# Handing the selection and the gates to the scheduler at 2.4 instead of 0.8 per attention step

## The chip, the cores and the metric

The kernel runs on one core of a Trainium2 chip. The metric is the device time of one execution in microseconds (us). The core's engines each work through an instruction queue of their own: TensorE (PE, with its weight loads as PEld), VectorE (DVE), ScalarE (ACT), GpSimd (POOL), and SyncE (SP), which here only issues transfers.

## What is computed

One encoder layer on 512 tokens of width 1024, in float32 throughout. Only the parts that stand near the change are told in detail.

```python
hn = rms_norm(h, g_mix)
c_q, c_kv, k_r, q_d, k_d, v_d = jnp.split(hn @ w_in, offs, axis=-1)
o_mla = mla_attention(...)          # 8 heads, full softmax over 512 keys
o_dil = dilated_attention(...)      # 8 heads, three dilated windows joined by their log sums
h = h + concat(rms_norm(o_mla), rms_norm(o_dil)) @ w_out
xn = rms_norm(h, g_ffn)
# PEER: per token and head two products with 128 keys each, top 16 of each,
# top 16 of the 256 sums, softmax: 8 x 16 experts out of 16384, with gates g
a = gelu(einsum('td,thkd->thk', xn, u_tab[eidx]))
h = h + einsum('thk,thkd->td', g * a, v_tab[eidx])
h = h + sigmoid(rms_norm(h, g_ple) @ w_gate) * (p @ w_proj)
out = rms_norm(h, g_final)
```

## The kernel before

The 512 tokens are four token tiles of 128. Tiles 1, 2 and 3 are "dense": for them all 16384 experts are computed, in 128 steps of 128 experts, and each hidden value is multiplied by a gate that is zero for experts that were not chosen. Tile 0 is the "gather" tile: its 128 chosen rows per token are fetched with indirect transfers and worked on by VectorE beside the dense steps.

The program has four stages in time:

1. The projections (to about 150 us in the trace).
2. The attention. A group is two heads of one token tile; there are 8 groups for a tile, 32 in all, in the tile order 1, 2, 3, 0. The generator `attention()` issues for each group the scores (L422 or L425), then the product with the values for the group three before (L466), the transposes for the group two before (L451) and the scaling of the weights, and yields after each of these four steps. After every yield the loop at L786 takes one step of `after(t)`, the work that follows a tile's attention, and then calls `fill(us)`.
3. `after(t)`: the output projection (L523, `mm<-wq,mT`), two adds per half into `ht` (L528), the norm (`ss`, a power on GpSimd at L141, then `hn`, L538 or L536), the transposes of `hn` (L545) with their copies `xTt`, the query projection (L562, `mm<-xTt,wq`), and the key products (L574), whose result `sc` goes to the selection. When it is through, it puts the tile's selection and, for a dense tile, four chunks of gates on the list `bg`.
4. The dense steps: hidden (L870, `h`), gelu and gates, values (L896, `y`). Steps 0 to 11 do tiles 1 and 2 only, while the gates of tile 3 are still being built; from step 12 on each step does three tiles, written out in a fixed order by hand.

The list `bg` is first in, first out. Its entries are generators: `topk(t)`, the selection (almost all on VectorE: maxima L589 and L598, their places L592 and L601, removal L595, the candidates L622, then the decoding and the one-hot products from L632 to L641; at its end three transposes on TensorE, L669 and L670), and `gates(t, c)`, which builds for 32 tokens the 128 by 128 table of gates: `hot` (L709) and `B` (L713) on VectorE for 8 tokens, 16 products on TensorE (L724), two copies into `stage` on ScalarE (L727), and at the end of a chunk one transfer of 2 MB to memory (`gD`, L729). `hot`, `B` and `stage` have two buffers each, and the products go to two PSUM buffers.

`fill(us)` takes steps from the head of `bg` until the costs that they name use up `us`. Those costs (1.6 for eight tokens of gates, for example) are numbers in the code, not measured times. A scheduler then orders the instructions of each engine, by the order in which the program issued them and by what is ready in its own model; on the chip every engine keeps that order. Two rules pull work forward whatever the rate is: three buffers `sc` exist, so `after` calls `fill` until enough halves of a selection are picked (L568), and before the dense steps everything on `bg` up to the gates of tile 3 is issued (L841). The gates of tile 3 are held back until then (`PRE`, `barred`).

Of the kernel before, what the change touches and what calls it, by code (L numbers as in the profile page):

```python
# [56 lines left out]
KE = 12  # L57
END = 10
NE, NX = 2, 4
FILL_A, FILL_B, FILL_D = 0.8, 3, 2  # L60
FILL_E = 2.2
PRE = ("gates", ORDER[2], 0)
ED = 2, 1, 0, 0
# [1146 lines left out]
```

## Time and profile before

| what | value |
|---|---|
| median of 3 runs | 1672.45 us (1669.31 to 1672.63) |
| the profiled execution's own time | 1674.36 us |
| span of that execution in the trace | 1672.3 us |
| TensorE busy | 1604.1 us (96% of the span) |
| VectorE busy | 1223.8 us (73%) |
| ScalarE busy | 737.5 us (44%) |
| GpSimd busy | 372.6 us (22%) |

The span is what the trace covers; the execution's own time is 2.06 us longer. Times in the trace count from the span's start. An engine's idle time is put down to the instruction that it waited for; matmuls are pipelined, so the start of one to the start of the next is its price, and the printed duration is longer. The granted clock of TensorE has two levels in this trace, 1.2 and 2.4 GHz, shown as 0.50 and 1.00.

### The profile page before, as it was taken

How to read it: one execution, taken by the hardware profiler on the slowest of the kernel's cores; microseconds unless marked ns; L12 is line 12 of the kernel's file. 1: busy time of each engine (PE TensorE's matmuls, PEld its weight loads, DVE VectorE, ACT ScalarE, POOL GpSimd, SP SyncE). 2: the span in 40 equal slices, each digit the busy share in tenths (PEclk: the TensorE clock that was granted, in tenths of full speed). 3: DMA queues.
4: the chain of work that ended last, by engine and by line, in shares of the span. 5: the costliest groups of instructions: out<-in, count | busy, mean ns of one | idle time of the engine just before them, and what ended most of it. 6: DMA issues, size and time to landing. Idle time of an engine off the chain costs nothing.

```text
span 1672.3 us, 24854 instructions
## 1 busy us (share of the span) xinstructions
PE 1604.1 (96%) x9369; PEld 1405.3 (84%) x9369; DVE 1223.8 (73%) x2495; ACT 737.5 (44%) x1220; POOL 372.6 (22%) x302
## 2 busy tenths in 40 slices
PE   7999999999679989999999999999999999999998
PEld 6776777778669889999999999999999999999877
DVE  5235468796999867787887887788888888864566
ACT  5435655645446544433333333333333333333455
POOL 1000000000000001044444444444444444300000
PEclk9999999999889999999999999999999999999999
DMA  7212254375867667599999999999999999975511
GB/s 240 62 52 95 82 172 133 114 239 206 298 248 243 233 216 265 185 309 327 324 321 323 309 334 321 324 316 339 320 312 313 334 322 323 319 269 200 182 58 51
DMA packets 154088, 402.73 MB, mean 241 GB/s; under 512 B 13168, under 2 KB 64496, under 8 KB 152432
## 3 DMA queue, kind: packets, MB, share of 16 engines
q1 hardware_dynamic: 115232, 241.48, 43.4%
q0 software_dynamic: 36864, 134.23, 23.3%
q10 hardware_dynamic: 1872, 25.43, 3.9%
q8 instruction: 73, 1.20, 0.3%
q14 instruction: 47, 0.39, 0.1%
HBM read 369.64 MB, written 31.46 MB: 240 GB/s over the span
## 4 chain that ended last, share of the span: by engine, by line
PE 82%; DVE 11%; ACT 2%; DMA 2%; issue 1%; POOL 1%; SPq 0%; POOLq 0%; DVEq 0%; ACTq 0%
PE y L896 31%; PE h L870 31%; PE mm L194 4%; PE mm L523 2%; PE mm L562 2%; PE pg L965 2%; PE po L466 2%; PE gq L724 2%; DVE B L713 1%; PE tp L451 1%; PE mm L425 1%; PE mm L422 1%; PE tp L250 1%; DVE rep L595 1%; DVE hot L709 1%
## 5 line engine op out<-in xcount | busy, mean ns | idle before, releaser
L870 PE MATMUL h<-xTh,lo 128*128 128x384 f32 (+1 forms) x1024 | 340.3, 332 | 0.8 <-ACT gt L673 0.8
L870 PE MATMUL h<-xTh,hi 128*128 128x384 f32 (+1 forms) x1024 | 340.1, 332 | 0.0
L870 PE MATMUL h<-xTl,hi 128*128 128x384 f32 (+1 forms) x1024 | 339.0, 331 | 0.0
L774 POOL DMA_INDIRECT row<-in_u_dram,ei x128 | 165.9, 1296 | 449.2 <-DVE row L762 241.4
L896 PE MATMUL y<-hi,wl 128*128 128x512 f32 x768 | 241.4, 395 | 8.5 <-DVE wl L885 8.5
L896 PE MATMUL y<-lo,wh 128*128 128x512 f32 x768 | 238.9, 392 | 0.0
L896 PE MATMUL y<-hi,wh 128*128 128x512 f32 x768 | 238.4, 392 | 0.0
L774 POOL DMA_INDIRECT row<-in_v_dram,ei x128 | 182.5, 1426 | 208.5 <-DVE h L768 170.1
L819 DVE TENSOR_TENSOR lo<-v,hi 128x1024 fp32r<-128x1024 f32 x140 | 171.5, 1225 | 73.4 <-ACT hi L817 72.8
L879 ACT ACTIVATE w<-h 128x384 f32<-128x384 f32 (+2 forms) x140 | 65.0, 464 | 361.6 <-PE h L870 346.6
L870 PEld LDWEIGHTS h<-xTh,lo 128*128 128x128 f32 x1024 | 193.8, 189 | 5.8 <-ACT gt L673 1.1
L870 PEld LDWEIGHTS h<-xTl,hi 128*128 128x128 f32 x1024 | 193.8, 189 | 4.7
L870 PEld LDWEIGHTS h<-xTh,hi 128*128 128x128 f32 x1024 | 193.5, 189 | 0.0
L819 DVE TENSOR_TENSOR lo<-u,hi 128x1024 fp32r<-128x1024 f32 x128 | 156.8, 1225 | 46.0 <-ACT hi L817 44.5
L817 ACT ACTIVATE hi<-v 128x1024 fp32r<-128x1024 f32 x140 | 148.2, 1058 | 94.2 <-PE y L896 94.0
L896 PEld LDWEIGHTS y<-lo,wh 128*128 128x128 f32 x768 | 144.7, 188 | 32.3
L896 PEld LDWEIGHTS y<-hi,wh 128*128 128x128 f32 x768 | 144.6, 188 | 31.7
L896 PEld LDWEIGHTS y<-hi,wl 128*128 128x128 f32 x768 | 141.3, 189 | 30.4 <-DVE wl L885 9.8
L768 DVE SCALAR_TENSOR_TENSOR h<-row,hh,h 128x1024 f32<-128x1024 f32 x128 | 164.2, 1283 | 2.9
L762 DVE SCALAR_TENSOR_TENSOR row<-row,xg 128x1024 f32<-128x1024 f32 x128 | 150.2, 1221 | 0.0
L883 ACT ACTIVATE wh<-w 128x384 fp32r<-128x384 f32 (+2 forms) x140 | 69.6, 497 | 180.4 <-DVE w L881 179.0
L817 ACT ACTIVATE hi<-u 128x1024 fp32r<-128x1024 f32 x128 | 133.9, 1046 | 1.6 <-PE h L870 1.6
(255 smaller groups left out, 2249.5 us busy)
## 6 DMA issues: line engine op xcount, KB each, us to landing
u<-in_uT_dram SPq DMA_DIRECT2D x140, 512.0 KB
v<-in_vB_dram SPq DMA_DIRECT2D x140, 512.0 KB
gD<-stage ACTq DMA_DIRECT2D x12, 2048.0 KB
g<-gD SPq DMA_DIRECT2D x29, 768.0 KB
wq<-in_w_out_dram SPq DMA_DIRECT2D x32, 512.0 KB
wq<-in_w_pq_dram SPq DMA_DIRECT2D x32, 512.0 KB
w<-in_w_in_dram SPq DMA_DIRECT2D x24, 256.0 KB
wg<-in_w_gate_dram SPq DMA_DIRECT2D x8, 512.0 KB
```

What stands on the lines that cost most here:

```text
L194: nc.tensor.matmul(acc[t], l[:, c, tok[t]], r, start=(c == 0 and k == 0), stop=(c == NC - 1 and k == 2))
L466: nc.tensor.matmul(cx[t]["po"][a * HD:(a + 1) * HD, hp, :], vv[:, grp, c, h * HD:(h + 1) * HD], st[g][a][:, c, :], start=(c == 0), stop=(c ...
L523: nc.tensor.matmul(pss[grp][:, q * P:(q + 1) * P], mT[grp][:, c, :], w[:, grp * 4 + c, :], start=(c == 0), stop=(c == 3))
L762: nc.vector.scalar_tensor_tensor(row, row, 1.0, xg, op0=OP.mult, op1=OP.mult, accum_out=hh[:, k:k + 1])
L768: nc.vector.scalar_tensor_tensor(h0, row, hh[:, k:k + 1], h0, op0=OP.mult, op1=OP.add)
L774: nc.gpsimd.indirect_dma_start(out=row, out_offset=None, in_=v if w else u, in_offset=bass.IndirectOffsetOnAxis(ap=eis[s][:, kk:kk + 1], a ...
L817: nc.scalar.activation(hi, w, AF.Copy)
L819: nc.vector.tensor_sub(lo, w, hi.bitcast(F32))
L870: nc.tensor.matmul(ps, l[:, cs], r[:, c, ts], start=(c == 0 and k == 0), stop=(c == NC - 1 and k == 2))
L879: nc.scalar.activation(w, ps, AF.Gelu)
L883: nc.scalar.activation(wh, w, AF.Copy)
L896: nc.tensor.matmul(y[n][s], l[:, ts], r[:, s * 512:(s + 1) * 512], start=(first and k == 0), stop=(last and k == 2))
```

## The change

One number: the budget with which `fill` is called after every step of the attention goes from 0.8 to 2.4.

```diff
 KE = 12
 END = 10
 NE, NX = 2, 4
-FILL_A, FILL_B, FILL_D = 0.8, 3, 2
+FILL_A, FILL_B, FILL_D = 2.4, 3, 2
 FILL_E = 2.2
 PRE = ("gates", ORDER[2], 0)
```

No instruction is added or removed; 140 weight tables, 768 gate products and all selections are the same. What changes is where they stand in each engine's queue. From tile 1's selection to the first dense steps the queues differ; before that, and from dense step 12 on, they read alike.

TensorE, where the normalised rows of token tile 2 are transposed (`hn`). `po` is the value product of the attention, `tp` the transposes of its weights, `mm<-xTt,wq` the query projection. Before:

```order
L466 MATMUL po<-prT,vv 64x128 x8
L545 MATMUL tp<-ident,hn 128x128 x8
L451 MATMUL tp<-ident,pr 128x128 x4
L562 MATMUL mm<-xTt,wq 128x128
```

And now (`gq<-ident,i1t` and `gq<-ident,gd` are the transposes that end the selection of tile 1, `gq<-hot,B` its gate products):

```order
L669 MATMUL gq<-ident,i1t 128x128 x2
L670 MATMUL gq<-ident,gd 128x128
L425 MATMUL mm<-kd,qd 128x512
L466 MATMUL po<-prT,vv 64x128 x8
L545 MATMUL tp<-ident,hn 128x128 x8
L724 LDWEIGHTS B
L724 MATMUL gq<-hot,B 128x128
```

Of the last two rows there are 80 pairs before the next transposes of the attention; then the attention, the query projection and the rest of the 256 gate products alternate. Before, the gate products of tile 1 began only a tile later, behind the attention of tile 0. The same pattern now comes a second time, for tile 2, after the transposes of tile 3.

VectorE at the same place, around `hn` of tile 2. `ss` leads to the norm, `xTt` are the two copies of its transposes, `e`, `ga`, `hot` and `B` belong to the gates. Before:

```order
L140 TENSOR_SCALAR ss<-ss 128x1
L538 TENSOR_SCALAR hn<-ht,ss 128x1024
L158 TENSOR_TENSOR xTt<-tp,gc 128x512 x2
L442 RECIPROCAL sm<-sm 128x2
L434 ISA pr,sm<-mm,bias_t 128x512
```

And now:

```order
L709 TENSOR_TENSOR hot<-ioh,ids 128x1024
L697 TENSOR_TENSOR e_2653<-io_1329,d_2624 128x256
L699 TENSOR_TENSOR e_2654<-ioh,d_2624 128x256
L702 TENSOR_TENSOR ga<-e_2653,g_2625 128x512
L538 TENSOR_SCALAR hn<-ht,ss 128x1024
L713 TENSOR_TENSOR B<-ga,e_2654 128x2048 x2
```

Between `hn` and the second copy `xTt` there now stand seven `B`, five `hot` and three sets of `e` and `ga`, where nothing stood.

VectorE near the end of the stage, at `after` of tile 0, the last tile: the adds into `ht` and what stands behind them. Before:

```order
L528 SCALAR_TENSOR_TENSOR ht_4067<-mm_4188,rg_2769,ht_4067 128x512
L639 TENSOR_TENSOR eq_4940<-eq_4940 128x8x128
L528 SCALAR_TENSOR_TENSOR ht_4067<-mm_4189,rg_2769,ht_4067 128x512
L709 TENSOR_TENSOR hot_4355<-ioh_1327,ids_4294 128x1024
L713 TENSOR_TENSOR B_4357<-ga_4351,e16_4350 128x2048
L709 TENSOR_TENSOR hot_4379<-ioh_1327,ids_4294 128x1024
L713 TENSOR_TENSOR B_4381<-ga_4351,e16_4350 128x2048
L140 TENSOR_SCALAR ss_4404<-ss_4404 128x1
```

And now (`cand`, `top` and `pos` belong to the second half of the selection of tile 3):

```order
L622 TENSOR_TENSOR cand<-vals 128x4x8
L528 SCALAR_TENSOR_TENSOR ht<-mm,rg,ht 128x512
L589 MAX top<-cand 128x8 x4
L592 MAX_INDEX pos<-top,cand 128x8 x4
L595 MATCH_REPLACE rep<-top,cand 128x80 x4
L598 MAX top<-rep 128x8 x4
L601 MAX_INDEX pos<-top,rep 128x8 x4
L528 SCALAR_TENSOR_TENSOR ht<-mm,rg,ht 128x512
```

In the first piece the adds of the second half of `ht` have gates of tile 2 around them. In the second the gates of tile 2 are gone from here (they are done a tile earlier), and the adds stand behind the selection of tile 3. On TensorE the output and the query projection of tile 0 then follow each other with no gate product in between: 64 instructions of L523, the 8 transposes of `hn`, 8 of L562, the transposes of the selection of tile 3, the other 56 of L562 with the 8 of L574, and the first 48 of L870.

## Rows read from the trace of the kernel before

**Rows 1.** The page, busy time: us, share of the span, instructions.

```profile
PE 1604.1 (96%) x9369; PEld 1405.3 (84%) x9369; DVE 1223.8 (73%) x2495; ACT 737.5 (44%) x1220; POOL 372.6 (22%) x302
```

**Rows 2.** Busy time by stretch (columns in the first line).

```profile
core 0: us, PE busy (x) PEld busy (x) DVE busy (x) ACT busy (x) POOL busy (x), PEclk, DMA share, GB/s
256.00:501.70 245.70, 210.34 (x1826) 179.62 (x1826) 208.10 (x842) 128.25 (x261) 8.90 (x8) 0.91 0.61 211
415.40:501.70 86.30, 60.61 (x559) 56.12 (x559) 83.97 (x331) 38.03 (x72) 1.64 (x2) 0.85 0.74 271
501.70:601.70 100.00, 94.85 (x736) 86.41 (x736) 78.81 (x132) 54.03 (x88) 0.00 (x0) 0.96 0.74 247
617.00:1540.00 923.00, 923.00 (x4669) 840.52 (x4669) 722.46 (x963) 345.35 (x456) 348.96 (x257) 1.00 0.89 304
```

**Rows 3.** TensorE in time: start, duration, instructions, idle before and its releaser.

```profile
289.13 1.06 PE L545 MATMUL tp<-ident,hn 128*128 128x128 f32 x8 [1.95 <-DVE hn L538]
...
431.40 9.36 PE L523 MATMUL mm<-wq,mT 128*128 128x128 f32 x64 [5.01 <-ACT d L677]
...
449.69 1.09 PE L545 MATMUL tp<-ident,hn 128*128 128x128 f32 x8 [0.56 <-DVE hn L536]
...
497.04 0.69 PE L669 MATMUL gq<-ident,i1t 128*128 128x128 f32 x2 [6.84 <-ACT i1t L651]
...
501.68 0.58 PE L870 MATMUL h<-xTh,lo 128*128 128x256 f32 x1 [0.81 <-ACT gt L673]
```

**Rows 4.** VectorE in time, gates of tile 1.

```profile
339.05 0.68 DVE L709 TENSOR_TENSOR hot<-ioh,ids 128x1024 f16<-128x1024 f16 x1
339.65 1.22 DVE L713 TENSOR_TENSOR B<-ga,e 128x2048 f16<-128x2048 f16 x1
340.79 0.16 DVE L442 RECIPROCAL sm<-sm 128x2 f32<-128x2 f32 x1
340.86 0.27 DVE L697 TENSOR_TENSOR e<-io,d 128x256 f16<-128x256 f16 x1
...
341.58 0.68 DVE L709 TENSOR_TENSOR hot<-ioh,ids 128x1024 f16<-128x1024 f16 x1
```

**Rows 5.** VectorE in time: the first half of a selection, begin and end.

```profile
234.05 0.87 DVE L589 MAX8 vals<-sc 128x8 f32<-128x128 f32 x4 [0.32 <-ACT sc L575]
...
258.68 0.28 DVE L641 TENSOR_TENSOR sel<-eq 128x128 f32<-128x128 bf16 x1
```

**Rows 6.** TensorE in time, attention and gates without waits.

```profile
345.51 1.12 PE L425 MATMUL mm<-kd,qd 64*128 64x512 f32 x2
...
346.98 1.09 PE L466 MATMUL po<-prT,vv 128*64 128x128 f32 x16
348.00 2.05 PE L523 MATMUL mm<-wq,mT 128*128 128x128 f32 x16
349.89 1.06 PE L724 MATMUL gq<-hot,B 128*128 128x128 f16 x16
350.79 1.04 PE L451 MATMUL tp<-ident,pr 128*128 128x128 f32 x8
351.67 1.95 PE L523 MATMUL mm<-wq,mT 128*128 128x128 f32 x16
```

**Rows 7.** GpSimd in time: two of the powers.

```profile
287.65 0.55 POOL L141 TENSOR_TENSOR ss<-ss,nhalf 128x1 f32<-128x1 f32 x1 [29.55 <-DVE ss L140]
...
332.48 3.53 POOL L484 TENSOR_TENSOR rg<-rg,nhalf 128x1 f32<-128x1 f32 x1 [34.33 <-DVE rg L483]
```

**Rows 8.** TensorE in time, in the first dense steps.

```profile
508.64 0.28 PE L870 MATMUL h<-xTl,hi 128*128 128x256 f32 x1
508.76 0.28 PE L870 MATMUL h<-xTh,hi 128*128 128x256 f32 x1
...
509.96 1.07 PE L724 MATMUL gq<-hot,B 128*128 128x128 f16 x16
```

**Rows 9.** The chain that ended last: start, duration, what.

```profile
584.32 9.95 DMA gD<-stage
```

## The prediction

> **What bounds the kernel now.** I began with the busy times of the page: TensorE works 96% of the span [rows 1]. The table by stretches shows where the rest is lost. From 617 to 1540 us TensorE is busy for all of the 923 us, so there nothing can be gained, and what comes earlier passes through whole: a start of the dense steps that moves by x moves the end by x. The stretch in which the change acts is 256 to 501.7 us: TensorE is busy 210.3 of 245.7 us and VectorE 208.1, so each stands idle for over 35 us, and the granted clock is 0.91 [rows 2]. Third, TensorE in time, from there to the first dense product at 501.68 [rows 3]. TensorE is held most in the last part, 415.4 to 501.7, where VectorE has hardly a gap (84.0 of 86.3 us) and TensorE only 60.6 us of work [rows 2]: it waits 5.0 us for the end of tile 2's selection and 6.8 us for that of tile 3 [rows 3]. That part is what the change relieves: gates of tile 2 leave it.
>
> **The change part by part.** No instruction comes or goes, so the sum is over waits. I walk the new order from 256 us to the first dense product, with start-to-start prices.
>
> Prices. On VectorE eight tokens of gates cost `hot` 0.60 and `B` 1.14, and a set of `e`, `e`, `ga` for sixteen 0.72 [rows 4]; a tile is 16 and 8 of them, 33.7 us. Half a selection took 24.6 us from 234.05 to 258.68, with six maxima of the attention and two copies at 0.6 each and small things inside, so 19 us alone [rows 5]. On TensorE 16 gate products cost 0.90, eight transposes 0.88, the value products of one group 1.02, a score product about 1, and eight instructions of the output or query projection 1.89, being two records each [rows 6]. A tile's output projection is then 15 us, its query projection 15, its 256 gate products 14.4.
>
> A. To the transposes of `hn` of tile 2, before at 289.1 [rows 3]. VectorE must now bring the selection of tile 1 to its end and begin `hot` before `hn`. From 234.05 its rows sum to 52.8 us up to `hn`'s end; with about 5 us of gaps, as it has there now, 291.9. Cost 2.8.
>
> B. The gates of tile 1. TensorE has 80 gate products (4.5 us) before its next transposes, and these need the PSUM tiles that the two `xTt` free. On VectorE seven `B`, five `hot` and three sets stand before the second `xTt`: with it 14.6 us, so 306.5, and TensorE stands idle about 9 of them. Then the relation turns: TensorE has 26.7 us (176 gate products 9.9, 32 projection instructions 7.5, four score products 3.9, 22 transposes 2.4, two groups' value products 2.0, the ones-product 0.9), VectorE only 21.1. With 2.5 us of small waits 335.7. Spread out, the gates would fill the gaps of both engines; in these two bursts each engine waits for the other in turn.
>
> C. To the ones-product (`tp<-ones,sq`, L482) that ends the tile's attention: VectorE has half a selection and five pairs of maxima and small rows, 24.5 us, TensorE 20.6: about 359.5.
>
> D. As A, for tile 3, without `hot` ahead of `hn`: TensorE 29.3 us and some 4 of waits, 393.
>
> E. As B, for tile 2: VectorE 18.4 us to `xTt`, then TensorE 24.3 and 2 of waits: 437.7.
>
> F. TensorE's rest of the attention and the first half of tile 0's output projection: 23.3 us and 1.5 of waits, 462.5. VectorE needs only 18.3 and waits.
>
> G. The second half of that projection is 7.5 us, but its two adds stand behind the selection of tile 3. From the first add to the end of `hn` VectorE has 24.6 us (40 rows of top-16 with their index loads 9.4, the candidates' 3.7, one-hot products 3.4, four adds 2.6, two `lo` 2.3, decoding and the rest 3.2), and the square and power before `hn` about 1: 488. TensorE stands idle for some 18 us. Before, its gap at this place was from the end of the projection that started at 431.40, about 440.8, to 449.69 [rows 3].
>
> H. TensorE from there to the first dense product: 20.1 us of work, 2.3 for copies on ScalarE, and about 3 for products at the lower clock after so long a gap: 513.4. Before it was 501.7, so 11.7 later.
>
> I. From there to the full steps. Before, the first 48 products took 8.3 us (501.68 to 509.96) instead of 48 times 0.12, which is 5.8, since the clock was still low after the wait [rows 3, 8]; now 20 us of work stand ahead and it should be high: a gain of 2.5. The remainder to 601.7 is TensorE's (94.9 of 100 us busy [rows 2]) with a transfer of 9.95 us at its end [rows 9], and is the same. All later stages cost nothing more: their order is the same, and their cover is a TensorE without gaps.
>
> Sum: 11.7 less 2.5 is 9.2 us. Against the profiled execution's own 1674.4 us that is 1683.6; this execution lies 1.9 above the median of the runs, 1672.45. I forecast 1681 for the median.
>
> Two things the trace of before doesn't price. The small waits in A to F (some 15 us of the sum) are taken from the stretches of before; if they vanish the start is 15 us earlier, if they double, 15 later. And GpSimd's power before `hn` took 0.55 us with VectorE idle beside it, but 3.53 us at 332.48, where VectorE ran `B` without a gap [rows 7]. In A and G it stands on the path; I take 0 to 3 us for each, and 0.5, since VectorE soon reaches `hn` itself and falls idle.
>
> The Trainium skill, SBUF — State Buffer, in the section SBUF: two separate sides, says that VectorE and GpSimd share a port pair as an exclusive lock, the loser being fully blocked. By it the power in A would wait behind `hot`, `hot`, `e`, `e` and `ga`, which read two SBUF inputs: up to 3 us, 1684 instead of 1681. The trace agrees as far as 3.53 against 0.55 us can show it.
>
> **The rivals.**
>
> 1. The holes of B, E and G cost more than the relieved end gives: the forecast, slower by 4 to 15 us.
>
> 2. Faster. VectorE's idle 37.6 us (245.7 less 208.1) is filled: its rows from 234.05 to the first add of tile 0 sum to 193 us, so 427 without any gap. If the bursts in B and E overlap so that VectorE's sum decides (21.1 and 20 us in place of 29.2 and 26.3), the first add comes 14 us sooner, at 448, the dense steps at 499, and with I the end is 5 us earlier: 1667. It decides if the first half of tile 0's output projection ends before 453 (513.4 less 462.5 is 50.9; 501.7 plus 2.5 less 50.9 is 453.3). For it speaks that both engines have 35 us free; against it, that each queue is in order and the new order puts like beside like.
>
> 3. No change: the waits come out about 9 us shorter than my sum, and what is gained at 440 to 501 is lost at 292 to 440.
>
> 4. A transfer becomes the wait. `stage` has two buffers, and a chunk's 2 MB need 9.95 us [rows 9]. A chunk of gates costs VectorE 8.4 us, and now nothing else spaces them. If they run at that price, the third and fourth chunk of each tile wait about 1.5 us, ScalarE's copies hold the PSUM tiles, and TensorE stands: four times 1.5, 6 us more, 1687. In my sum a chunk takes about 11 us, which hides it; it decides from a chunk time below 10 us.
>
> That the new number does nothing is excluded: the order shows the gates of tile 1 ahead of the query projection of tile 2, and TensorE follows its order.
>
> **How the numbers follow.** The forecast 0.52, rival 4 0.12, no change 0.16, faster 0.20. A measurement of this kernel tells about 0.2% (3.3 us) from no change. Slower is then 0.64, same 0.16, faster 0.20. The range goes from 1661, six beyond rival 2 for gaps of VectorE that A keeps and that may close too, to 1699, the forecast with the small waits doubled and one power of 3 us: with either end about a tenth is left out.
>
> **What would show it.** Right: TensorE shows a gap of 5 us or more after the transposes of `hn` of tiles 2 and 3, waiting for `B` or `xTt`; one of 12 us or more before those of tile 0, waiting for `hn`; and the first dense product stands at 508 to 518 us at the high clock, with the full steps about 100 us later. The stretch 415 to 501 has fewer gate products and VectorE gaps in it. Wrong: the first half of tile 0's output projection ends before 453 us; or the gap at tile 0's `hn` is short because VectorE was ahead; or ScalarE's `stage` waits for `gD`.

## The result, and the profile after

The change made the kernel slower: 1688.12 us (median of 4 runs, 1686.68 to 1689.42) against 1672.54 (4 runs), a ratio of 1.0094 with a 95% interval of 1.0074 to 1.0114. The profiled execution took 1687.50 us, its span is 1685.7; against the profiled execution of before that is 13.1 us more.

TensorE in time (start, duration, instructions, idle before and its releaser), the rows that answer to [rows 3] and to steps A to H:

```profile
256.81 1.05 PE L482 MATMUL tp<-ones,sq 128*128 128x1 f32 x8 [0.88 <-ACT prT L456]
...
291.29 1.94 PE L545 MATMUL tp<-ident,hn 128*128 128x128 f32 x8 [3.08 <-DVE hn L538]
...
305.84 1.33 PE L451 MATMUL tp<-ident,pr 128*128 128x128 f32 x5 [3.35 <-DVE xTt L158]
...
361.49 0.95 PE L482 MATMUL tp<-ones,sq 128*128 128x1 f32 x8
...
392.15 1.09 PE L545 MATMUL tp<-ident,hn 128*128 128x128 f32 x8
...
395.10 1.07 PE L724 MATMUL gq<-hot,B 128*128 128x128 f16 x16 [1.86 <-DVE B L713]
...
407.93 1.33 PE L451 MATMUL tp<-ident,pr 128*128 128x128 f32 x5 [3.95 <-DVE xTt L158]
...
454.81 7.31 PE L523 MATMUL mm<-wq,mT 128*128 128x128 f32 x64
469.54 10.07 PE L523 MATMUL mm<-wq,mT 128*128 128x128 f32 x64 [7.42 <-DMA wq<-in_w_out_dram]
489.68 1.97 PE L545 MATMUL tp<-ident,hn 128*128 128x128 f32 x8 [10.07 <-DVE hn L536]
...
514.40 0.39 PE L870 MATMUL h<-xTh,lo 128*128 128x256 f32 x1 [0.69 <-ACT sc L575]
```

The two bursts are there. Between the transposes of `hn` of tile 2 (291.29) and the next transposes of the attention (305.84) lie 14.6 us. TensorE waits for 6.1 of them, in four pieces; the rest is eight transposes and 80 gate products, at a granted clock of 0.74. For tile 3, from 392.15 to 407.93, it waits for 7.9 of 15.8 us, in five pieces, at 0.86. The longest piece of each is the one for `xTt`. At tile 0 it waits twice, 7.4 us for weights and 10.1 for `hn`. The first dense product stands at 514.4, before at 501.68 [rows 3].

VectorE at the first burst: `hn`, the first two `B` behind it, and the two copies `xTt`, 14 us later.

```profile
290.40 0.74 DVE L538 TENSOR_SCALAR hn<-ht,ss 128x1024 f32<-128x1024 f32 x1
291.06 2.35 DVE L713 TENSOR_TENSOR B<-ga,e 128x2048 f16<-128x2048 f16 x2
...
305.10 1.28 DVE L158 TENSOR_TENSOR xTt<-tp,gc 128x512 f32<-128x512 f32 x2
```

The stretches that answer to [rows 2] (columns in the first line):

```profile
core 0: us, PE busy (x) PEld busy (x) DVE busy (x) ACT busy (x) POOL busy (x), PEclk, DMA share, GB/s
256.00:415.00 159.00, 138.31 (x1166) 112.43 (x1167) 138.18 (x523) 93.53 (x197) 2.74 (x5) 0.91 0.48 168
...
415.00:501.70 86.70, 67.75 (x583) 61.84 (x580) 65.54 (x284) 33.88 (x63) 1.68 (x3) 0.86 0.76 263
...
617.00:1540.00 923.00, 923.00 (x4664) 840.19 (x4664) 725.05 (x991) 344.92 (x455) 347.86 (x256) 1.00 0.89 305
```

VectorE, which was busy for nearly all of 415 to 501 before [rows 2], is now idle for 21 of 86.7 us there. TensorE is busy for 67.8 us of it, before for 60.6, yet it reaches the first dense product 12.7 us later. The dense stretch is as it was: TensorE without a gap, so the delay passes through.

### The profile page after: what moved, and what is told of

Read it like the earlier page. It is cut to its first block, busy times and chain, and to the rows that moved or that the text cites. A ratio compares the mean times of both kernels' runs of the same rounds, so it can differ in the third digit from the quotient of the medians.

```text
span 1685.7 us, 24863 instructions
## 1 busy us (share of the span) xinstructions
PE 1611.3 (96%) x9369; PEld 1410.3 (84%) x9369; DVE 1224.0 (73%) x2495; ACT 738.9 (44%) x1220; POOL 367.6 (22%) x302
## 4 chain that ended last, share of the span: by engine, by line
PE 84%; DVE 9%; ACT 3%; DMA 2%; issue 1%; POOL 1%; SPq 0%; POOLq 0%; DVEq 0%; ACTq 0%
PE y L896 31%; PE h L870 30%; PE mm L194 4%; PE mm L562 3%; PE mm L523 3%; PE gq L724 2%; PE po L466 2%; PE pg L965 2%; PE tp L451 2%; PE mm L425 1%; PE mm L422 1%; DVE B L713 1%; PE tp L250 1%; PE h L873 1%; DVE hot L709 1%
## 5 line engine op out<-in xcount | busy, mean ns | idle before, releaser
L870 PE MATMUL h<-xTh,lo 128*128 128x384 f32 (+1 forms) x1024 | 339.0, 331 | 0.7 <-ACT sc L575 0.7
L870 PE MATMUL h<-xTh,hi 128*128 128x384 f32 (+1 forms) x1024 | 339.1, 331 | 0.0
L870 PE MATMUL h<-xTl,hi 128*128 128x384 f32 (+1 forms) x1024 | 338.0, 330 | 0.0
L870 PEld LDWEIGHTS h<-xTh,lo 128*128 128x128 f32 x1024 | 192.6, 188 | 5.8 <-ACT sc L575 1.1
L870 PEld LDWEIGHTS h<-xTl,hi 128*128 128x128 f32 x1024 | 192.5, 188 | 4.7
L870 PEld LDWEIGHTS h<-xTh,hi 128*128 128x128 f32 x1024 | 192.4, 188 | 0.0
L896 PEld LDWEIGHTS y<-hi,wl 128*128 128x128 f32 x768 | 141.6, 189 | 30.8 <-DVE wl L885 10.1
```

The lines of the kernel that those rows point to most:

```text
L870: nc.tensor.matmul(ps, l[:, cs], r[:, c, ts], start=(c == 0 and k == 0), stop=(c == NC - 1 and k == 2))
L896: nc.tensor.matmul(y[n][s], l[:, ts], r[:, s * 512:(s + 1) * 512], start=(first and k == 0), stop=(last and k == 2))
```

## The experiments

All start from the changed kernel (rate 2.4). Each has two measures: its time against runs of the kernel before on the same chip, and in its profile the stage from the ones-product near 256 us (`tp<-ones,sq`, the end of tile 2's attention, up to which the queues read nearly alike) to the first dense product. That stage took 245.8 us before (255.84 to 501.68) and 257.6 after (256.81 to 514.40). The start of it, and the end of tile 0's attention, in the kernel before:

```profile
255.84 1.05 PE L482 MATMUL tp<-ones,sq 128*128 128x1 f32 x8 [0.89 <-ACT prT L456]
...
415.40 1.05 PE L482 MATMUL tp<-ones,sq 128*128 128x1 f32 x8 [0.69 <-ACT sq L472]
```

The runs of the kernel before that stood beside an experiment had medians of 1672.3 to 1674.4 us, so times are compared by the ratio. The stage is read from one execution of each kernel: e9 has the queues of the changed kernel up to the end of the attention and reached that point 2.9 us later, so differences of some 3 us in this column may be the execution's.

| run | stage us | median us | ratio to before, interval |
|---|---|---|---|
| before, rate 0.8 | 245.8 | 1672.5 | |
| after, rate 2.4 | 257.6 | 1688.1 | 1.0094 [1.0074, 1.0114] |
| e1 no bursts | 241.4 | 1667.1 | 0.9958 [0.9944, 0.9972] |
| e2 2.4 early only | 244.2 | 1671.0 | 0.9974 [0.9960, 0.9988] |
| e5 burst E only | 250.0 | 1676.7 | 1.0031 [1.0013, 1.0049] |
| e6 burst B only | 245.6 | 1673.9 | 1.0010 [0.9994, 1.0026] |
| e7 one table load later | 260.3 | 1687.3 | 1.0087 [1.0055, 1.0120] |
| e9 tables behind the weights | 260.7 | 1685.8 | 1.0075 [1.0052, 1.0098] |
| e8 e1, half of tile 2's gates at the end | 235.9 | 1662.9 | 0.9946 [0.9924, 0.9968] |
| e10 e8 and e9 together | 231.7 | 1660.4 | 0.9926 [0.9902, 0.9951] |
| e12 rate 1.0 | 234.1 | 1663.8 | 0.9942 [0.9925, 0.9959] |
| e3 rate 1.2 | 230.2 | 1657.5 | 0.9897 [0.9874, 0.9920] |
| e11 rate 1.4 | 236.7 | 1663.4 | 0.9940 [0.9917, 0.9963] |
| e4 rate 1.6 | 231.8 | 1661.1 | 0.9922 [0.9892, 0.9953] |

**e1, no bursts.** The same rate, but from the first output product of a dense tile until its `xTt` is issued no gates are handed over, so nothing of them stands between `hn` and `xTt`.

```diff
     barred = [PRE]
+    quiet = []
-        while us > 0 and bg and bg[0][0] not in barred:
+        while us > 0 and bg and bg[0][0] not in barred and bg[0][0][0] not in quiet:
...
         nc.sync.dma_start(ht, x[tok[t], :])
+        if t in DENSE:
+            quiet.append("gates")
...
             nc.sync.dma_start(xd[t], xTt)
+            quiet.clear()
```

> The rate stays 2.4, but gates are not handed over from the first output product of a dense tile until the copies `xTt` of its `hn` are issued; so no `hot` and `B` stand between `hn` and `xTt`, and the 80 gate products in a row behind the transposes of `hn` are gone. Theory (the two bursts B and E, then the queue G on VectorE): TensorE loses its waits for `B` and `xTt` behind the transposes of tiles 2 and 3 (about 9 us each), the ones-product that ends tile 2's attention comes at about 352 instead of 361.5, the first half of tile 0's output projection ends at 446 to 454 instead of 462, the gap before `hn` of tile 0 stays (some 17 us), the first dense product stands at 498 to 506 and the time is 1672 to 1680. Rival 'amount' (what costs is how much VectorE work lies in the attention, wherever it stands): the same 1686 to 1690. Rival 'end' (the loss is the gap before `hn` of tile 0 alone): the first dense product stays at 512 to 515, since VectorE has the same rows up to there, 1685 to 1689.

The ones-product at 361.5 us that this text and three later ones call tile 2's is the one that ends tile 3's attention; `after` of tile 2 runs beside that attention.

TensorE in time (an edit shifts line numbers: L548 here is L545 of the changed kernel):

```profile
291.60 1.06 PE L548 MATMUL tp<-ident,hn 128*128 128x128 f32 x8 [0.79 <-DVE hn L541]
293.01 0.66 PE L452 MATMUL tp<-ident,pr 128*128 128x128 f32 x4 [0.35 <-DVE xTt L158]
...
357.88 1.05 PE L483 MATMUL tp<-ones,sq 128*128 128x1 f32 x8 [0.28 <-ACT prT L457]
...
434.78 0.95 PE L483 MATMUL tp<-ones,sq 128*128 128x1 f32 x8
...
454.03 9.46 PE L526 MATMUL mm<-wq,mT 128*128 128x128 f32 x64 [7.75 <-DMA wq<-in_w_out_dram]
472.84 1.97 PE L548 MATMUL tp<-ident,hn 128*128 128x128 f32 x8 [9.35 <-DVE hn L539]
```

The attention's transposes follow those of `hn` after 1.4 us instead of 14.6, the end of the attention (434.78) is 16.7 us earlier than in the changed kernel (451.48), and the gap G is untouched: 7.8 and 9.4 us. The stage is 16.2 us shorter, the time is below the expected 1672 to 1680 and below the kernel before. The rivals 'amount' and 'end' fall: all the rows of VectorE are the same, only their place is not. The ones-product that ends tile 3's attention came only 3.6 us earlier, not 9; more of B's price showed behind it (e5).

**e5 and e6, one burst each.** The hold of e1 for one tile only. Against e1, e5 reads as follows; e6 has `ORDER[2]` in its place.

```diff
-        if t in DENSE:
+        if t == ORDER[1]:
             quiet.append("gates")
```

> Rate 2.4; gates are held from the output projection to `xTt` for tile 2 only, so burst B is gone and burst E stays. In the run without both, the ones-product of tile 2 came 3.6 us earlier than in the changed kernel, the transposes of `hn` of tile 3 6.5, the end of the attention 16.7 and the first dense product about 17. Theory (each burst has its own price, B 6.5 us and E 10): end of the attention at 445, first dense product at 507 to 509, 1679 to 1683. Rival 'the last decides' (VectorE's backlog is carried to E, so one burst left costs nearly all): first dense product at 511 to 514, 1684 to 1688.

> Rate 2.4; gates held for tile 3 only, so burst B stays and burst E is gone. Theory (own prices): the ones-product of tile 2 at 361, the transposes of `hn` of tile 3 at 392, the end of the attention at 441, first dense product at 503 to 506, 1673 to 1678. Rival 'the last decides': first dense product at 497 to 500, 1667 to 1670.

TensorE in time, e5:

```profile
385.25 1.06 PE L548 MATMUL tp<-ident,hn 128*128 128x128 f32 x8
388.84 3.24 PE L728 MATMUL gq<-hot,B 128*128 128x128 f16 x32 [2.53 <-DVE B L717]
...
402.49 0.69 PE L452 MATMUL tp<-ident,pr 128*128 128x128 f32 x2 [4.56 <-DVE xTt L158]
...
506.38 0.39 PE L874 MATMUL h<-xTh,lo 128*128 128x256 f32 x1 [0.69 <-ACT sc L579]
```

and e6:

```profile
308.59 1.33 PE L452 MATMUL tp<-ident,pr 128*128 128x128 f32 x5 [3.41 <-DVE xTt L158]
...
505.15 0.39 PE L874 MATMUL h<-xTh,lo 128*128 128x256 f32 x1 [0.69 <-ACT sc L579]
```

Taking B away shortens the stage by 7.6 us, taking E away by 12.0, both together by 16.2; by the ratios of the runs it is 10.5, 14 and 23 us. So each burst has its own price. Whether the two overlap is not shown: the 3.4 us by which the single prices exceed the joint one are about what two executions of one order can differ by. e5's time is 2 us below the expected range, e6's is in it; 'the last decides' falls.

**e2, the high rate for the first half only.**

```diff
         for g in range(NG + 4):
+            FILL_A = 2.4 if g < 26 else 0.8
```

> The rate is 2.4 up to group 25 of the attention (the selection and the gates of tile 1) and 0.8 from group 26 on. So burst B is as in the changed kernel, burst E and the queue G are not there: the selection of tile 2 ends and its gates come beside the last output projection, as in the kernel before. Theory (each burst costs by itself): up to the ones-product of tile 2 nothing changes against the changed kernel (361 us), the transposes of `hn` of tile 3 have no wait behind them, and the end of the stage has the work that it had before; the first dense product at 508 to 518, 1681 to 1690. Rival 'end': with G gone nearly all of the loss is gone, first dense product at 500 to 504, 1671 to 1676. Rival 'amount': half of the loss, 1678 to 1682.

```profile
421.37 1.05 PE L482 MATMUL tp<-ones,sq 128*128 128x1 f32 x8
422.28 0.41 PE L670 MATMUL gq<-ident,i1t 128*128 128x128 f32 x2
...
501.62 0.58 PE L871 MATMUL h<-xTh,lo 128*128 128x256 f32 x1 [0.81 <-ACT gt L674]
```

My expectation missed, and the numbers are those of the rival 'end', though not by its reason (e1 had G in full and was faster still). I had left the end of the stage at its 86.3 us of before; it took 80.3 (421.37 to 501.62), because the selection of tile 2 now ends with the attention, at 422, and nobody waits for it (before, 5.0 us [rows 3]). The end of the attention is 6.0 us later than before (421.37 against 415.40), and these 6 us come back behind it. Burst B is in this run, with 14.7 us from the transposes of `hn` of tile 2 to the next of the attention (293.52 to 308.18); behind those of tile 3 it is 1.4 us (393.29 to 394.73). So the high rate does bring a gain, even with one burst in it; the two bursts of the changed kernel take more than it.

**e7 and e9, the weights of the output projection.** The wait of 7.4 us for them was not in my prediction. e7 moves one load (u, 512 KB) that stood ahead of them in SyncE's queue; e9 hands over all the first loads for the dense steps eight steps later, by which 2 MB of them (two u, two v) stand behind the second half of the weights in SyncE's queue.

```diff
-    for m in range(UB - 1):
-        load_tab(uT, m, "u")
+    load_tab(uT, 0, "u")
...
+    load_tab(uT, 1, "u")
     while bg and bg[0][0] != PRE:
```

In e9 the lines that issue `gf`, both `xt`, two u, two v and the split of u are moved into `prefetch()` (cut here):

```diff
...
     while afters:
         step_after()
+        n_after += 1
+        if n_after == 8:
+            prefetch()
         fill(FILL_B)
```

> The changed kernel with the load of the second table of u issued behind the last query projection instead of ahead of the output weights of tile 0; in SyncE's queue these weights then no longer stand behind a load that waits for its buffer. Theory (VectorE decides G; the wait of 7.4 us for the weights is hidden by it): TensorE's wait for `wq` is gone or below 2 us, the wait before `hn` of tile 0 grows to 15 to 18 us, its transposes stay at 488 to 491 and the first dense product at 513 to 516, 1685 to 1690. Rival 'transfer' (the weights were late and all of G hangs on them): transposes at 482, first dense product at 507, 1679 to 1682.

> The run with the second u table moved left the wait for the output weights at 6.9 us: they were issued 5 us earlier and landed no earlier, because 3 MB were under way before them. Here the first loads for the dense steps are handed over after eight steps of the work that follows tile 0's attention; of them 2 MB (u and v) now stand behind the second half of the output weights in SyncE's queue, 1.5 MB still ahead. Theory (VectorE decides G, the wait for the weights is hidden): that wait falls from 7.4 to 2 to 4 us and the wait before `hn` of tile 0 grows by as much; from the ones-product at 256.8 to the first dense product it is 256 to 259 us as in the changed kernel (257.6), 1685 to 1690. Rival 'transfer': 252 to 254 us, 1681 to 1684.

e7, TensorE in time, and the transfers of 455 to 475 us in 40 slices:

```profile
471.08 10.33 PE L523 MATMUL mm<-wq,mT 128*128 128x128 f32 x64 [6.92 <-DMA wq<-in_w_out_dram]
493.33 1.97 PE L545 MATMUL tp<-ident,hn 128*128 128x128 f32 x8 [11.92 <-DVE hn L536]
```

```profile
GB/s 270 270 385 213 205 197 188 238 287 369 401 401 410 401 434 401 418 418 377 426 401 426 393 418 401 410 410 426 401 418 401 401 279 180 156 107 74 49 25 25
```

e9, TensorE in time (the view ends within the second group, which has 8):

```profile
466.72 9.01 PE L523 MATMUL mm<-wq,mT 128*128 128x128 f32 x64 [1.93 <-DMA wq<-in_w_out_dram]
492.74 1.54 PE L545 MATMUL tp<-ident,hn 128*128 128x128 f32 x6 [17.01 <-DVE hn L536]
```

e7 settled nothing on G: the wait for the weights, expected below 2 us, was 6.9. They were issued 5 us earlier (458.83 against 463.77) and landed no earlier, with 3 MB issued just ahead of them and the transfers at some 410 GB/s. e9 did: the wait for weights falls to 1.9 us, the one for `hn` grows to 17.0, and from the end of the attention to the first dense product it is 63.1 us (454.15 to 517.25) against 62.9 in the changed kernel. VectorE decides G; the late weights are hidden. The changed kernel's own trace says the same: from the first add of tile 0 (464.57) to the transposes of `hn` (489.68) VectorE is busy for 24.8 of 25.1 us. (The stage of e9, 260.7 us, is longer than the 256 to 259 expected; the excess comes from ahead of the edit, see the last section.)

**e8 and e10, something left for the gap.** e1, with half of tile 2's gates held until the attention is through; e10 adds the edit of e9.

```diff
-    barred = [PRE]
+    barred = [PRE, ("gates", ORDER[1], 2)]
...
     att_s.close()
+    barred.pop()
```

> As the run without bursts, and the last two of the four chunks of tile 2's gates are held until the attention is through; the selection of tile 3 stands behind them, so the adds of tile 0 don't stand behind that selection and TensorE has 128 gate products to fill G with. Theory (what G costs is the order: selection ahead of the adds and no gate products): no wait for `hn` of tile 0 above 4 us, VectorE without gaps from the end of the attention on; the first dense product at 480 to 492 with the wait for the selection of tile 3 ahead of it, 1651 to 1663. Rival 'nothing gained' (VectorE is the bound of the end anyway, so its order doesn't matter): first dense product at 496 to 498, 1665 to 1669.

> No bursts, half of tile 2's gates held for the end, and the first loads for the dense steps handed over later as well. In the run without the last part VectorE itself waited 4.8 us for gate products that stood behind the wait for the weights (5.6 us), so there that wait should be on the path. Theory: that wait 1 to 3 us, from the ones-product at 257 to the first dense product 231 to 234 us instead of 235.9, 1657 to 1661. Rival (VectorE's sum decides there as well): unchanged, 235 to 237 us, 1661 to 1665.

e8, VectorE, then TensorE of e8 and of e10:

```profile
452.12 0.69 DVE L713 TENSOR_TENSOR hot<-ioh,ids 128x1024 f16<-128x1024 f16 x1 [4.76 <-PE gq L728]
```

```profile
447.46 2.93 PE L526 MATMUL mm<-wq,mT 128*128 128x128 f32 x12 [5.59 <-DMA wq<-in_w_out_dram]
467.95 1.97 PE L548 MATMUL tp<-ident,hn 128*128 128x128 f32 x8 [7.96 <-DVE hn L539]
```

```profile
442.65 1.60 PE L526 MATMUL mm<-wq,mT 128*128 128x128 f32 x12 [1.68 <-DMA wq<-in_w_out_dram]
462.11 1.97 PE L548 MATMUL tp<-ident,hn 128*128 128x128 f32 x8 [10.01 <-DVE hn L539]
```

Half of the gates for the end shortens the stage by 5.5 us against e1; the first dense product at 492.8 is 0.8 above the expected range and the time at its upper end, and the wait for `hn` did not go as I had said. Here the weights are on the path: gate products stand behind them on TensorE, and VectorE waits 4.8 us for a free `hot`. With the loads later the stage loses another 4.2 us, as expected. The times go the same way, but less clearly: the intervals of e1, e8 and e10 overlap each other. The same wait is free in the changed kernel and costs here, since the queue behind it feeds VectorE: its wait for `hot` falls from 4.8 us in e8 to 1.7 in e10.

**e3, e4, e11, e12: the rates between.** One number each (`FILL_A` 1.2, 1.6, 1.4, 1.0).

> Rate 1.2. The order has the gate products of tile 1 in groups of 16 between attention and projection, from the middle of tile 2's query projection on, none directly behind the transposes of `hn`; all gates of tile 2 stand at the end, beside the output and query projection of tile 0, as before, and the selection of tile 2 ends 32 output products earlier than before. Theory (the bursts cost, not the rate): the waits of 7 us for `xTt` don't appear, the end of the stage has some 10 us less of VectorE's work in it, the first dense product stands at 490 to 499, 1661 to 1671, faster than both kernels. Rival 'amount': between the two kernels, 1675 to 1681. Rival 'no effect' (what is done earlier is lost elsewhere): 1671 to 1675.

> Rate 1.6. As at 1.2 the gate products stand in groups of 16; the selection of tile 1 now ends right behind the transposes of `hn` of tile 2 and a quarter of tile 2's gates comes before the last output projection; 96 gate products still stand right before the transposes of `hn` of tile 0, so TensorE has work there. Theory: no wait for `xTt` over 4 us, first dense product at 488 to 498, 1660 to 1671. Rival 'amount': 1679 to 1685. If the selection of tile 1 in front of the scores' work on VectorE costs as A does, 3 us more.

> Rate 1.4. The order has the gate products of tile 1 in groups of 16 from tile 2's query projection on, the selection of tile 2 in the middle of tile 3's query projection, and four fifths of tile 2's gates at the end, beside the output projection of tile 0. Theory (any rate at which no burst stands behind `hn` is better than 0.8, and best is the one that leaves gate products for the gap at the end): 1655 to 1662. Rival 'narrow' (1.2 was a lucky order): 1664 to 1674.

> Rate 1.0. The selection of tile 1 ends within tile 2's query projection, that of tile 2 right behind the end of the attention, gate products of tile 1 in groups of 16. Theory: the selection of tile 2 out of the last projection is what relieves the end most, so most of the gain of 1.2 is there already: 1657 to 1664. Rival 'narrow': 1665 to 1672, between the kernel before and 1.2 or no better than before.

e3, TensorE in time:

```profile
412.17 0.41 PE L669 MATMUL gq<-ident,i1t 128*128 128x128 f32 x2
...
454.36 1.97 PE L545 MATMUL tp<-ident,hn 128*128 128x128 f32 x8 [0.17 <-DVE hn L536]
...
485.26 0.69 PE L669 MATMUL gq<-ident,i1t 128*128 128x128 f32 x2 [4.12 <-ACT i1t L651]
486.97 0.58 PE L870 MATMUL h<-xTh,lo 128*128 128x256 f32 x1 [0.81 <-ACT gt L673]
```

All four are faster than 0.8 by 0.6 to 1.0%, and 1.2, at 1657.5 us better than I had expected (1661 to 1671), is the fastest of this study. At 1.2 no gate product stands behind `hn` of tiles 2 and 3, the selection of tile 2 ends with the attention, and all of tile 2's gates are left for the end, so the transposes of tile 0 wait 0.2 us for `hn`, not 10. 'Amount' falls for good: every rate from 1.0 to 1.6 is faster than 0.8, and 2.4 is slower. Where between 1.6 and 2.4 it turns was not run. 1.4 missed its expectation by 1.4 us; it is slower than 1.2 in every run, and from 1.6 not apart (the runs overlap). Its `hn` of tile 0 was held by GpSimd (last section) and TensorE waited 6.7 us for the weights. 1.0 ends with a wait of 7.9 us for the selection of tile 3, where 1.2 has 4.1.

## Why the prediction was right, and where not

| step | predicted | measured |
|---|---|---|
| A transposes of `hn`, tile 2 | 291.9 | 291.3 |
| B next transposes of the attention | 306.5 | 305.8 |
| B last gate products of tile 1 end | 335.7 | 336.7 |
| C ones-product that ends tile 3's attention | 359.5 | 361.5 |
| D transposes of `hn`, tile 3 | 393 | 392.2 |
| E next transposes of the attention (393 and 18.4) | 411.4 | 407.9 |
| E last gate products of tile 2 end | 437.7 | 437.1 |
| F first half of tile 0's projection ends | 462.5 | 462.1 |
| G `hn` of tile 0 | 488 | 489.6 |
| H first dense product | 513.4 | 514.4 |
| I full steps after it | 100.0 less 2.5 | 97.9 |

- The forecast, slower by the holes of B, E and G, came, and by its mechanism. The walk along the new order holds to 2 us at every step but the middle of E. There the stretch to `xTt` took 15.8 us, not 18.4, and the one behind it 29.2, not 26.3; that the end of E fits is luck, two errors against each other. (Before, the gate products of tile 1 began at 336.2 us, just behind the end of tile 3's attention, and not behind that of tile 0, as is said ahead of the prediction.)
- The signs that were named came in kind, but two not in size. Behind tiles 2 and 3 TensorE waits for `B`, `xTt` and ScalarE's copies into `stage`, in pieces of at most 3.35 and 3.95 us, where one of 5 or more was named. The wait for `hn` of tile 0 is 10.1 us, where 12 or more was named. The first dense product is at the high clock (granted 1.00 from 514.4 to 520), and from 415 to 501.7 the trace has 137 products into `gq`, before 262. None of the signs of being wrong came.
- B's length is right, and its filling is not: the prediction had TensorE idle for about 9 us at full speed, measured are 6.1 of waits and a granted clock of 0.74. VectorE's queue set the length, so this did not show in the time.
- B and E were shown by taking them away (e1, e5, e6): 16 us of the stage, against a loss of 12.7 at the first dense product. Without them the change is a gain.
- G has the right end and a wrong picture: one gap of 18 us was forecast, measured are 7.4 for weights and 10.1 for `hn`. The step had no transfer in it: I read SyncE's loads nowhere. It cost nothing, because VectorE was the later one (24.6 us forecast, 24.8 busy; e9), and in e8 it was worth about 4.
- The size is 7 us short: 1681 forecast for the median, 1688.1 measured. The full steps begin 10.6 us later than before where 9.2 were forecast, 1.0 of the 1.4 by G and H, 0.4 by I. The first full step, which the prediction held equal, ran longer at the low clock, 7.1 us to the next step (granted 0.56), before 6.3 (0.64), which makes the delay 11.4 us. Another 2.0 us fell in the tail (last section), where nothing was forecast: 13.4 of span. The medians lie 15.6 apart, since the profiled execution of before was above its median and that of after is 0.6 below its own. Two of the prediction's figures are below their own terms: C's give 360.2, and 1683.6 less 1.9 is 1681.7. The first full step after, and before:

```profile
612.32 1.22 PE L896 MATMUL y<-hi,wl 128*128 128x512 f32 x2 [4.62 <-DVE wl L885]
```

```profile
601.72 1.22 PE L896 MATMUL y<-hi,wl 128*128 128x512 f32 x2 [4.46 <-DVE wl L885]
```

- GpSimd's power in A and G, 0 to 3 us each: `ss` took 0.55 and 0.59 us here.

```profile
286.80 0.55 POOL L141 TENSOR_TENSOR ss<-ss,nhalf 128x1 f32<-128x1 f32 x1 [25.48 <-DVE ss L140]
...
487.72 0.59 POOL L141 TENSOR_TENSOR ss<-ss,nhalf 128x1 f32<-128x1 f32 x1 [34.38 <-DVE ss L140]
```

So the value taken, 0.5, was right for this order, and only for it. In A the power was over at 287.35 us, ahead of the first `hot` at 288.12, so the wait behind `hot`, `e` and `ga`, which the prediction priced at up to 3 us, did not come up there.
- Rival 2 (faster, when the bursts overlap) was the state that e1 made: first half of the projection done at 446.3 (439.76 and 6.52 us), below the named 453, first dense product at 497.7 (named 499), 1667.1 us (named 1667). What decided between the two was whether gates are handed over from a tile's first output product to its `xTt`.
- Rival 4 (`stage` waits for the transfer of a chunk) did not come: from 285 to 440 us ScalarE's 64 copies into `stage` wait for gate products alone, 24 times.

## What to carry to other kernels

When background work is moved earlier on engines with queues in order, look at where it lands, not at how much it is: work of one kind in a run, put between a producer and the copy that the next engine waits for, makes both engines wait in turn, though each has time to spare. A hold around that place kept the high rate and turned a loss of 0.9% into a gain of 0.4%. And leave some of the filler for the last gap: at the best rate here, 1.2, all gates of tile 2 were left for it. But 1.4, between two rates that are as good or better, shows that the exact order counts as well, so try the neighbours too.

## What the runs showed of the hardware

- A power of 128 values on GpSimd took 0.55 us in most places and 6.92 in e11, right ahead of `hn` of tile 0, for as long as VectorE ran `e`, `ga`, `hot` and `B` from 455.76 to 462.33:

```profile
455.82 6.92 POOL L141 TENSOR_TENSOR ss<-ss,nhalf 128x1 f32<-128x1 f32 x1 [34.32 <-DVE ss L140]
```

```profile
462.77 1.28 DVE L536 SCALAR_TENSOR_TENSOR hn<-ht,ss,gf 128x1024 f32<-128x1024 f32 x1 [0.44 <-POOL ss L141]
```

My bound of 3 us was less than half of that. The Trainium skill, SBUF — State Buffer, in the section SBUF: two separate sides, says that a VectorE instruction with two SBUF inputs and a GpSimd instruction that reads SBUF hold the port pair as an exclusive lock, and that the other one fully blocks. The trace agrees (`e`, `ga`, `hot` and `B` each read two SBUF tiles), and it shows one GpSimd instruction kept out over eleven VectorE instructions in a row, not one.

- The granted clock fell at places that the order does not fix. In the tail of the changed kernel a wait of 1.67 us was followed by products at half speed, 3.51 us instead of 1.95 (granted 0.57 from 1605 to 1609):

```profile
1603.04 0.50 PE L965 MATMUL pg<-gh,xTl 128*128 128x512 f32 x1 [1.67 <-ACT gh L958]
...
1605.15 3.51 PE L873 MATMUL h<-x,u 128*128 128x128 f32 x16
```

The same place before, where the clock stayed at 1.00:

```profile
1591.14 0.49 PE L965 MATMUL pg<-gh,xTl 128*128 128x512 f32 x1 [1.19 <-ACT gh L958]
...
1593.20 1.95 PE L873 MATMUL h<-x,u 128*128 128x128 f32 x16
```

Such slow products stand in the tail of nine of the fourteen profiled executions (after, e1, e2, e5, e6, e7, e9, e10, e12; 2.54 to 3.51 us), and not in before, e3, e4, e8 and e11. At the place shown they were slow in seven, and in these TensorE had waited longer ahead of them (1.24 to 2.20 us) than in the other seven (0.93 to 1.19). And e9, whose queues are the changed kernel's up to 450 us, ran 361 to 366 us at a clock of 0.57, behind a wait of 1.2 us, where the changed kernel had 1.00, and lost 3 us by that; from 352 to 356 us it was the other way round, 1.00 and 0.57. So 2 of the 13.4 us of the profiled pair may belong to the execution and not to the change; why the waits differ from one execution to another stays open.
